# A hybrid decoder layer on one core: parked quarters of x in the idle k/q buffer, staggered block loads, and an in-place block inverse

## The chip, the core and the metric

The kernel runs on one core of a Trainium2 chip. The core has five engines with instruction streams of their own: TensorE (PE in the profile; its weight loads are PEld), VectorE (DVE), ScalarE (ACT), GpSimd (POOL) and SyncE (SP). Here SP and POOL mainly issue DMAs. The engines wait for one another through semaphores; within one engine the stream runs in order. The metric is device microseconds of one execution, lower is better.

## What is computed

One layer of a decoder trunk in float32, for a prompt of 1024 rows and 8 sample rows of 1024 channels. The reference, cut to its core:

```python
h = rmsnorm(x, norm_pre) * (1.0 + scale[:, None]) + shift[:, None]
proj = h @ w_in                                     # 1024 -> 10256 columns
hA, cA, bA, zA, qkv, zB, beta_raw, alpha_raw, gA, gB = jnp.split(proj, offs, axis=-1)
a_conv, new_buf_a = causal_dwconv(cA * hA, buf_a, conv_a_w)
yA = ((bA * a_conv) * jax.nn.silu(zA)) @ w_out_a
qkv_c, new_buf_b = causal_dwconv(qkv, buf_b, conv_b_w)
q, k, v = jnp.split(jax.nn.silu(qkv_c), [D_K, 2 * D_K], axis=-1)     # 8 heads of 128
...
a_mat = jnp.where(strict, jnp.einsum('bhncd,bhnsd->bhncs', kb, k) * decay, 0.0)
a_mat = a_mat + jnp.eye(C, dtype=jnp.float32)
sol = lax.linalg.triangular_solve(a_mat, rhs, left_side=True, lower=True, unit_diagonal=True)
...                                                 # a scan over the chunks of one head
o = rmsnorm(o, onorm_w) * jax.nn.silu(zB)
yB = o @ w_out_b
merged = jax.nn.sigmoid(gA) * yA + jax.nn.sigmoid(gB) * yB
y = x + gate[:, None] * rmsnorm(merged @ w_o, norm_post)
```

## The kernel before

**Stages.** (1) A startup computes the modulation and the normalised, transposed input x, kept in SBUF as a high and a low part, `xh` and `xl` (8 tiles of 128 channels by 1032 columns). Every product takes three matmuls (high by high, low by high, high by low). (2) Eight heads: for each head the jobs k, q, v, two gates and zB, each one 128-column slice of `w_in` against all of x, in three column groups. Beside them runs the delta rule of the head: `decay_gen`, `delta_gen`, and `sample_gen` for the sample rows. (3) Three groups of branch A, four jobs each. (4) `products()`: the five other groups of branch A as seven products each (P1, P2, P6, P7, P4, P5, P3) on quarters of x, a Strassen-like scheme. P1 and P2 read x as it stands; P6, P7 and P4 read the "parked" quarter combinations T2, T3 and T4 of x, and P5 reads T1, all of which `quarter_gen` computed and stored to the DRAM scratch `txs` during the heads. (5) The output products and the final norm.

**Order of the work.** The program text is written by a planner at build time. PE's jobs run in a fixed order; everything else is a "strand", a Python generator. After each matmul triple `slot()` (line 599) steps every strand whose model time lies behind PE's. `force(cond)` (line 612) steps strands with no matmul of the job between them until a condition holds. The tile framework then orders each engine's stream by readiness in a model of its own, with the place in the text as the priority, and sets the semaphores.

**Slots.** `T4` is a pool of `NT4 = 5` buffers of 128 by 1056 floats (class `Slots`, line 629), handed out first in, first out. During the heads these take slots: v of a head (`vT`), the split of k and q (`kqh`, `kql`, per half), the block inverse (`At`, `Tt`), the output `yb`, one gate row (`gate`, by `take`, which forces), the sample state (`S0`, `rB`), and `quarter_gen` (`qa`, `qb`, `qhi`, `qlo`). A strand that finds too few slots yields and asks again later.

**The block inverse.** `delta_gen` (line 864) stores the 32 by 32 diagonal blocks of a head to DRAM (`sA`) and reads all 32 of them back, one block a partition, into `At`. `Tt` is set to the identity by GpSimd, and 31 steps of two VectorE instructions each (`Ttmp` is the product) do a forward substitution. The result goes through DRAM (`sT`) into `Tn`, and matmuls then join the blocks into `U`. The chunk loop follows: eight chunks, each a chain between TensorE, ScalarE and VectorE, whose output gathers in `on`.

**Flags.** Head h's `delta_gen` begins once head h-2 is out ("out": its row of yB is stored), and its chunk loop once head h-1 is out. "done" is set earlier, when a head's chunk loop has ended. The buffer `kq` (k and q of a head) exists twice; k of head h waits for "done" of head h-2, and for heads 0 and 1 for nothing.

**Loads of the parked quarters.** `block_load` (line 1458) loads T2, T3 and T4, four DMAs each, from POOL into slots (`tx`) of the pool that takes over the heads' memory, and then T1 into the second half of `xh` and `xl`. The weights of the products come by DMAs from SP (`wr`).

In the profile nearly all instructions stand under one line, L122, the planner's wrapper; so instructions are told apart by the names of their tiles.

Of the kernel before, what the change touches and what calls it, by code (L numbers as in the profile page):

```python
# [8 lines left out]
F32 = mybir.dt.float32  # L9
# [3 lines left out]
ALU = mybir.AluOpType  # L13
# [3 lines left out]
P = 128  # L17
D = 1024
NK = 8
S = 1024  # L20
NB = 8
NT = S + NB
NH = 8
C = 128
NC = S // C
# [4 lines left out]
CY = S + 4 * NB  # L30
# [2 lines left out]
COL_H, COL_C, COL_B, COL_Z, COL_Q, COL_K, COL_V = 0, 1024, 2048, 3072, 4096, 5120, 6144  # L33
COL_ZB, COL_BA, COL_GA, COL_GB = 7168, 8192, 8208, 9232
BIG = 1.0e30
NT4 = 5
DYN = 2048
HT = NT // 2
PW = HT // 2
# [115 lines left out]
def hybrid_step(  # L155
# [23 lines left out]
    def tt(out, a, b, op):  # L179
        V.tensor_tensor(out=out, in0=a, in1=b, op=op)  # L180
# [7 lines left out]
    def stt(out, a, s, b, op0, op1):  # L188
        V.scalar_tensor_tensor(out=out, in0=a, scalar=s, in1=b, op0=op0, op1=op1)
# [64 lines left out]
    egc = cpool.tile([P, NC, NH], F32, name="egc")  # L254
# [14 lines left out]
    sA = dram.tile([NH, NC, 4, 32, 32], F32, name="sA")  # L269
# [334 lines left out]
    def start(gen):  # L604
        bg.append(Strand(gen, sched.cur.t if sched.cur else sched.clk["PE"]))
# [59 lines left out]
    def when(*conds):  # L665
        while not all(c() for c in conds):
            yield
# [124 lines left out]
    flags = {}  # L792
# [70 lines left out]

    def delta_gen(h, st):
        ch = lambda a: a[:, :, h:h + 1]
        while "DA" not in st or "v" not in st or (h > 1 and not flags.get(("out", h - 2))):
            yield
        kq, vT, gcB, DB, DA = st["kq"], st["v"], st["gcB"], st["DB"], st["DA"]
        V.tensor_copy(out=qs_s[:, h, :, 0], in_=smpl(kq[:, 0, :]))
# [7 lines left out]
        ssq = bp.tile([P, NC], F32, tag="ssq", name="ssq", bufs=2)  # L877
# [18 lines left out]
        rk = rsqrt(bp, ssk, P, NC, "rk")  # L896
        cB = bp.tile([P, NC], F32, tag="cB", name="cB", bufs=2)
        nx = bp.tile([P, NC], F32, tag="nx", name="nx", bufs=2)
        vs = bp.tile([P, NC], F32, tag="vs", name="vs", bufs=2)
        bh = beta[:, 0:NC, h]  # L900
        tt(vs, rk, bh, ALU.mult)
        tt(cB, vs, rk, ALU.mult)
        stt(nx, cB, -1.0, egc[:, :, h], ALU.mult, ALU.mult)
        yield

        for half in range(2):
# [25 lines left out]
        for b in range(4):  # L932
            sched.loose(b < 3)
            bs = slice(32 * b, 32 * b + 32)
            SY.dma_start(out=sA[h, :, b].rearrange("c r j -> r c j"), in_=DB[bs, :, bs])
        while not T4.ready(2):
            yield
        At_, Tt_ = T4.get("At", S), T4.get("Tt", S)
        At = At_[:32].rearrange("p (r j) -> p r j", j=32)
        Tf = Tt_[:32]  # L940
        Tt = Tf.rearrange("p (r j) -> p r j", j=32)
        tmp = bp.tile([32, 272], F32, tag="Ttmp", name="Ttmp")
        SY.dma_start(out=At, in_=sA[h].rearrange("c b r j -> (c b) r j"))
        sched.loose()
        GP.memset(Tf, 0.0)
        GP.memset(Tf[:, 0:1024:33], 1.0)
        sched.loose(False)
        t_at, sched.cur.t = sched.cur.t, t_kk
        vp = bp.tile([P, NC, C], F32, tag="vp", name="vp", bufs=2)
        for half in range(2):  # L950
# [14 lines left out]
        yield  # L965
        sched.cur.t = max(sched.cur.t, t_at)
        yield 0.0
        for j in range(31):
            n, w = 31 - j, j + 1
            tv = tmp[:, 0:n * w].rearrange("p (n w) -> p n w", w=w)  # L970
            tt(tv, At[:, j + 1:32, j:j + 1].to_broadcast([32, n, w]),
               Tt[:, j:j + 1, 0:w].to_broadcast([32, n, w]), ALU.mult)
            tt(Tt[:, j + 1:32, 0:w], Tt[:, j + 1:32, 0:w], tv, ALU.subtract)
            yield 0.0
        SY.dma_start(out=sT[h].rearrange("c b r j -> (c b) r j"), in_=Tt)
        T4.give(At_)
# [25 lines left out]
        for p in (0, 1):  # L1002
            b1 = slice(64 * p, 64 * p + 32)
            b2 = slice(64 * p + 32, 64 * p + 64)
            pt = ps_aux().rearrange("p (c j) -> p c j", j=64)
            for c in range(NC):
                PE.matmul(pt[b1, c, 0:32], lhsT=Tn[b1, c, :], rhs=Qs[b1, c, 0:32], start=True, stop=True)
            if p:
                A.mul(out=U[b1, :, b2], in_=pt[b1, :, 0:32], mul=-1.0)
# [6 lines left out]
            A.mul(out=U[b1, :, b2], in_=pt[b1, :, 0:32], mul=-1.0)  # L1016
            A.mul(out=T11[b2, :, 0:32], in_=pt2[b2, :, 0:32], mul=-1.0)
            yield 0.0
        pt = ps_aux().rearrange("p (c j) -> p c j", j=64)
        for c in range(NC):  # L1020
# [7 lines left out]
        A.mul(out=U[0:64, :, 64:128], in_=pt[0:64], mul=-1.0)  # L1028
# [48 lines left out]
        yield  # L1077
        tt(on, on, ro.unsqueeze(2).to_broadcast([P, NC, C]), ALU.mult)
        yield
        while "sz" not in st or not T4.ready():  # L1080
            yield
        sz = st["sz"]
        yb = T4.get("yb", S)
        for half in range(2):
            pt = ps_aux()
            for i in range(4):
# [4 lines left out]
            yield  # L1091
        sched.join("V")
        store(yBsc[h, :, 0:S], yb)
        T4.give(yb)
        flags[("out", h)] = True

    def head_jobs(h):
# [31 lines left out]
    L = []  # L1129
# [211 lines left out]
            yield  # L1341


    def quarter_gen():
        for k in range(4):
            yield from when(lambda: T4.ready(2))
            a, b = T4.get("qa", NT), T4.get("qb", NT)
            a1, a2, b1, b2 = a[:, 0:HT], a[:, HT:NT], b[:, 0:HT], b[:, HT:NT]
            tt(a, xh[:, k, :].bitcast(F32), xl[:, k, :].bitcast(F32), ALU.add)
            yield  # L1350
            tt(b, xh[:, 4 + k, :].bitcast(F32), xl[:, 4 + k, :].bitcast(F32), ALU.add)
            yield
            tt(a1, a2, a1, ALU.subtract)
            tt(a2, b2, a2, ALU.subtract)
            yield
            tt(b2, b2, a1, ALU.subtract)
            tt(b1, b1, b2, ALU.subtract)
            yield
            for r, v in enumerate((a, b)):
                yield from when(lambda: T4.ready(2))  # L1360
                hi, lo = T4.get("qhi", NT), T4.get("qlo", NT)
                A.copy(out=hi.bitcast(F32R), in_=v)
                yield
                tt(lo.bitcast(F32R), v, hi, ALU.subtract)
                T4.give(v)
                store(txs[r, 0, k].bitcast(F32), hi)
                store(txs[r, 1, k].bitcast(F32), lo)
                T4.give(hi)
                T4.give(lo)
                yield  # L1370
# [135 lines left out]
    def products():  # L1506
# [6 lines left out]
        for t in range(SG, NK):  # L1513
            tiles = [L[0].take("acc", NT) for _ in range(4)]
            for p in PROD:
# [284 lines left out]
```

## Time and profile before

| | us |
|---|---|
| median of 3 runs (lowest, highest) | 1494.98 (1494.11, 1499.9) |
| the profiled execution, whole | 1496.61 |
| its span, first to last instruction | 1494.6 |
| TensorE busy in the span | 1423.4 (95%) |
| VectorE busy | 947.8 (63%) |
| ScalarE busy | 645.1 (43%) |
| GpSimd busy | 42.0 (3%) |

The views used below: the page's 40 slices give the busy share in tenths; the table of stages gives, for each stretch, its length, then busy us (and instructions) of PE, PEld, DVE, ACT and POOL, then the granted TensorE clock, the DMA share and GB/s; the timeline gives start, length, engine, line, operation, written and read tiles, sizes, and in brackets the idle time before the instruction and what ended it; the view of a tile gives shortest, median and longest instruction in ns and the first and last start in us.

### The profile page before, as it was taken

What the parts mean: (1) busy time and instruction counts of PE and PEld (TensorE: products, weight loads), DVE (VectorE), ACT (ScalarE), POOL (GpSimd) and SP (SyncE); (2) the same over time, 40 slices, a digit from 0 to 9 for tenths busy, and PEclk for the clock granted to TensorE, in tenths of its full rate; (3) what the DMA queues carried; (4) which work ended last, traced back from release to release, by engine and by line L of the source; (5) the groups of instructions that cost most, each with busy time, mean ns of one, the idle gap of its engine ahead of it and who ended that gap; (6) DMA issues with size and microseconds to landing.
All of it is one profiled execution on the core that took longest, in us unless ns stands there. A gap on an engine that the chain in (4) does not pass through costs nothing.

```text
span 1494.6 us, 25637 instructions
## 1 busy us (share of the span) xinstructions
PE 1423.4 (95%) x10050; PEld 1362.3 (91%) x10050; DVE 947.8 (63%) x2391; ACT 645.1 (43%) x1512; POOL 42.0 (3%) x73
## 2 busy tenths in 40 slices
PE   6999959989999999999999999959999999999997
PEld 4899959979999999999999999959999989999786
DVE  6865868849559578595776824227767773444553
ACT  6765634645547438465383332112323462332221
POOL 0000000000000001000000000020000000000000
PEclk9999979989999999999999999979999999999999
DMA  9624222214332322223222312094121474451221
GB/s 321 165 60 145 89 79 80 79 54 159 92 84 77 96 75 80 79 80 100 65 80 66 89 52 73 15 308 112 48 71 58 139 257 138 155 166 42 89 85 57
DMA packets 182542, 155.42 MB, mean 104 GB/s; under 512 B 25405, under 2 KB 161063, under 8 KB 182414
## 3 DMA queue, kind: packets, MB, share of 16 engines
q1 hardware_dynamic: 177900, 145.26, 32.5%
q0 software_dynamic: 4320, 8.46, 1.8%
q8 instruction: 79, 1.29, 0.3%
q14 instruction: 41, 0.34, 0.1%
q10 hardware_dynamic: 202, 0.08, 0.0%
HBM read 117.08 MB, written 36.91 MB: 103 GB/s over the span
## 4 chain that ended last, share of the span: by engine, by line
PE 75%; DVE 10%; DMA 7%; ACT 4%; SPq 2%; issue 2%; DVEq 0%; ACTq 0%
PE pm_t L122 57%; PE pa_t L122 16%; SPq L122 2%; DVE kq L122 2%; DMA gcB<-gsc 2%; PE pb L122 2%; DVE Tt L122 2%; DVE Ttmp L122 2%; DVE wlo L122 1%; DMA xs<-in_x_prompt_dram 1%; ACT junk L122 1%; DMA aw<-in_ada_w_dram 1%; ACT L122 1%; DMA txs<-qlo 1%; DVE vT L122 1%
## 5 line engine op out<-in xcount | busy, mean ns | idle before, releaser
L122 PE MATMUL pm_t<-xh,whi 128*128 128x344 f32 (+1 forms) x1576 | 520.6, 330 | 18.8 <-ACT gate L122 17.1
L122 PE MATMUL pm_t<-xh,wlo 128*128 128x344 f32 (+1 forms) x1576 | 500.7, 318 | 0.6 <-DVE wlo L122 0.6
L122 PE MATMUL pm_t<-xl,whi 128*128 128x344 f32 (+1 forms) x1576 | 499.8, 317 | 0.0
L122 PEld LDWEIGHTS pm_t<-xh,whi 128*128 128x128 f32 x1576 | 298.8, 190 | 21.7 <-ACT gate L122 17.7
L122 PEld LDWEIGHTS pm_t<-xh,wlo 128*128 128x128 f32 x1576 | 297.9, 189 | 1.1 <-DVE wlo L122 0.9
L122 PEld LDWEIGHTS pm_t<-xl,whi 128*128 128x128 f32 x1576 | 298.5, 189 | 0.1
L122 DVE TENSOR_TENSOR wlo<-wraw,whi 128x512 fp32r<-128x512 f32 x152 | 102.1, 683 | 61.5 <-ACT whi L122 61.2
L122 ACT CAST whi<-wraw 128x512 fp32r<-128x512 f32 x152 | 91.5, 622 | 105.2 <-PE pm_t L122 104.9
L122 PE MATMUL pm_t<-ylo,whi 128*128 128x344 f32 x384 | 123.4, 321 | 1.8 <-DVE ylo L122 1.8
L122 PE MATMUL pm_t<-yhi,whi 128*128 128x344 f32 x384 | 123.2, 322 | 0.6 <-DVE acc L122 0.6
L122 PE MATMUL pm_t<-yhi,wlo 128*128 128x344 f32 x384 | 123.6, 322 | 0.0
L122 DVE TENSOR_TENSOR Ttmp<-At,Tt 32x31 f32<-32x31 f32 (+15 forms) x248 | 81.4, 328 | 7.0 <-DMA At<-sA 2.2
L122 DVE TENSOR_TENSOR Tt<-Tt,Ttmp 32x31 f32<-32x31 f32 (+15 forms) x248 | 81.7, 329 | 5.1
L122 PEld LDWEIGHTS pm_t<-ylo,whi 128*128 128x128 f32 x384 | 72.6, 189 | 2.2 <-DVE ylo L122 2.1
L122 PEld LDWEIGHTS pm_t<-yhi,whi 128*128 128x128 f32 x384 | 72.7, 190 | 1.2 <-issue 0.8
L122 PEld LDWEIGHTS pm_t<-yhi,wlo 128*128 128x128 f32 x384 | 72.6, 189 | 0.0
L122 DVE SCALAR_TENSOR_TENSOR kq<-raw,vecs,kq 128x528 f32<-128x528 f32 x96 | 69.6, 757 | 1.3 <-ACT kq L122 1.1
L122 PE MATMUL pm_t<-tx,whi 128*128 128x258 f32 x256 | 48.3, 291 | 18.0 <-ACT whi L122 18.0
L122 ACT CAST whi<-wr 128x1024 fp32r<-128x1024 f32 x26 | 27.3, 1049 | 79.9 <-PE pm_t L122 37.3
L122 PEld LDWEIGHTS pm_t<-tx,whi 128*128 128x128 f32 x256 | 41.1, 197 | 18.2 <-issue 18.2
L122 ACT ACTIVATE junk<-pa_t 128x128 f32<-128x128 f32 x192 | 53.9, 281 | 8.5 <-PE pa_t L122 5.6
L122 ACT COPY vn<-pa_t 128x128 f32<-128x128 f32 x64 | 17.1, 267 | 84.3 <-PE pa_t L122 83.9
(367 smaller groups left out, 2575.7 us busy)
## 6 DMA issues: line engine op xcount, KB each, us to landing
wraw<-in_w_in_dram SPq DMA_DIRECT2D x60, 512.0 KB
wr<-in_w_in_dram SPq DMA_DIRECT2D x36, 256.0 KB
aw<-in_ada_w_dram SPq DMA_DIRECT2D x16, 512.0 KB
tx<-txs POOLq DMA_DIRECT2D x12, 516.0 KB, 12.4
txs<-qhi SPq DMA_DIRECT2D x8, 516.0 KB
txs<-qlo SPq DMA_DIRECT2D x8, 516.0 KB
gBsc<-gate SPq DMA_DIRECT2D x8, 516.0 KB
gAsc<-gate SPq DMA_DIRECT2D x8, 516.0 KB
```

Source lines behind the costliest of these rows:

```text
L122: r = f(*args, **kw)
```

## The change

- `NT4` goes from 5 to 6. The output `on` of the chunk loop is no buffer of its own any more; it takes a slot, and `yb` is written into the same slot, which goes back when the row is stored.
- `quarter_gen` no longer takes slots for its two combinations: it is given one of the two `kq` buffers (the one that head 1 takes later), is started before the job that follows the startup instead of after the beta/alpha product, and takes slots for `qhi` and `qlo` only.
- The block inverse works in place: the sign moves into `cB`, the blocks are loaded straight into `Tt`, there are 30 steps, each one column narrower, and VectorE sets the diagonal in the middle. `At` and the two GpSimd memsets are gone, and three `A.mul` by -1 become copies.
- `delta_gen` of head h begins on "done" of head h-2, and its chunk loop on "out" of head h-2 and a free slot. `ssq` has three buffers.
- `block_load` asks for T2, T3, T4 and T1 not before units 0, 1, 2 and 3 of the products (`unit[0]` counts products).
- The load of yB rows for the output product starts one product earlier (at P6 of the last group, not P7).

```diff
-NT4 = 5
+NT4 = 6
...
-        while "DA" not in st or "v" not in st or (h > 1 and not flags.get(("out", h - 2))):
+        while "DA" not in st or "v" not in st or (h > 1 and not flags.get(("done", h - 2))):
...
-        tt(cB, vs, rk, ALU.mult)
-        stt(nx, cB, -1.0, egc[:, :, h], ALU.mult, ALU.mult)
+        stt(cB, vs, -1.0, rk, ALU.mult, ALU.mult)
+        tt(nx, cB, egc[:, :, h], ALU.mult)
...
-        while not T4.ready(2):
+        while not T4.ready():
             yield
-        At_, Tt_ = T4.get("At", S), T4.get("Tt", S)
-        At = At_[:32].rearrange("p (r j) -> p r j", j=32)
+        Tt_ = T4.get("Tt", S)
...
-        SY.dma_start(out=At, in_=sA[h].rearrange("c b r j -> (c b) r j"))
-        sched.loose()
-        GP.memset(Tf, 0.0)
-        GP.memset(Tf[:, 0:1024:33], 1.0)
-        sched.loose(False)
+        SY.dma_start(out=Tt, in_=sA[h].rearrange("c b r j -> (c b) r j"))
...
-        for j in range(31):
-            n, w = 31 - j, j + 1
-            tv = tmp[:, 0:n * w].rearrange("p (n w) -> p n w", w=w)
-            tt(tv, At[:, j + 1:32, j:j + 1].to_broadcast([32, n, w]),
-               Tt[:, j:j + 1, 0:w].to_broadcast([32, n, w]), ALU.mult)
-            tt(Tt[:, j + 1:32, 0:w], Tt[:, j + 1:32, 0:w], tv, ALU.subtract)
+        for j in range(1, 31):
+            n = 31 - j
+            tv = tmp[:, 0:n * j].rearrange("p (n w) -> p n w", w=j)
+            tt(tv, Tt[:, j + 1:32, j:j + 1].to_broadcast([32, n, j]),
+               Tt[:, j:j + 1, 0:j].to_broadcast([32, n, j]), ALU.mult)
+            tt(Tt[:, j + 1:32, 0:j], Tt[:, j + 1:32, 0:j], tv, ALU.add)
+            if j == 15:
+                sched.loose()
+                V.memset(Tf[:, 0:1024:33], 1.0)
+                sched.loose(False)
             yield 0.0
...
-        while h and not flags.get(("out", h - 1)):
-            yield
-        on = bp.tile([P, NC, C], F32, tag="on", name="on")
+        while (h > 1 and not flags.get(("out", h - 2))) or not T4.ready():
+            yield
+        on_ = T4.get("on", S)
+        on = on_.rearrange("p (c d) -> p c d", d=C)
...
-        yb = T4.get("yb", S)
+        yb = on_
...
-    def quarter_gen():
+    def quarter_gen(q_):
         for k in range(4):
-            yield from when(lambda: T4.ready(2))
-            a, b = T4.get("qa", NT), T4.get("qb", NT)
+            a, b = q_[:, 0, 0:NT], q_[:, 1, 0:NT]
...
-        for b, r, cs in (("T2", 1, slice(HT, NT)), ("T3", 0, slice(HT, NT)), ("T4", 1, slice(0, HT))):
-            yield from when(lambda: L, lambda: L[0].ready(4))
+        for i, (b, r, cs) in enumerate((("T2", 1, slice(HT, NT)), ("T3", 0, slice(HT, NT)), ("T4", 1, slice(0, HT)))):
+            yield from when(lambda: L, lambda: L[0].ready(4), lambda: unit[0] >= i)
...
+        yield from when(lambda: unit[0] >= 3)
         for part, x_ in enumerate((xh, xl)):
...
-                    if p == "P7":
+                    if p == "P6":
                         start(load_rows("yb", yBsc))
...
+    start(quarter_gen(bp.tile([P, 2, CY], F32, tag="kq", name="kqq", bufs=2)))
     jobs[0][6]()
...
-    start(quarter_gen())
```

More of the change, by code (lines that the diff above doesn't have):

```diff
@@ L876, in delta_gen @@
         ssk = bp.tile([P, NC], F32, tag="ssk", name="ssk", bufs=2)
-        ssq = bp.tile([P, NC], F32, tag="ssq", name="ssq", bufs=2)
+        ssq = bp.tile([P, NC], F32, tag="ssq", name="ssq", bufs=3)
         for src, sq in ((0, ssk), (1, ssq)):
@@ L935, in delta_gen @@
             SY.dma_start(out=sA[h, :, b].rearrange("c r j -> r c j"), in_=DB[bs, :, bs])
-        while not T4.ready(2):
+        while not T4.ready():
             yield
-        At_, Tt_ = T4.get("At", S), T4.get("Tt", S)
-        At = At_[:32].rearrange("p (r j) -> p r j", j=32)
+        Tt_ = T4.get("Tt", S)
         Tf = Tt_[:32]
         Tt = Tf.rearrange("p (r j) -> p r j", j=32)
-        tmp = bp.tile([32, 272], F32, tag="Ttmp", name="Ttmp")
-        SY.dma_start(out=At, in_=sA[h].rearrange("c b r j -> (c b) r j"))
-        sched.loose()
-        GP.memset(Tf, 0.0)
-        GP.memset(Tf[:, 0:1024:33], 1.0)
-        sched.loose(False)
+        tmp = bp.tile([32, 256], F32, tag="Ttmp", name="Ttmp")
+        SY.dma_start(out=Tt, in_=sA[h].rearrange("c b r j -> (c b) r j"))
         t_at, sched.cur.t = sched.cur.t, t_kk
@@ L967, in delta_gen @@
         yield 0.0
-        for j in range(31):
-            n, w = 31 - j, j + 1
-            tv = tmp[:, 0:n * w].rearrange("p (n w) -> p n w", w=w)
-            tt(tv, At[:, j + 1:32, j:j + 1].to_broadcast([32, n, w]),
-               Tt[:, j:j + 1, 0:w].to_broadcast([32, n, w]), ALU.mult)
-            tt(Tt[:, j + 1:32, 0:w], Tt[:, j + 1:32, 0:w], tv, ALU.subtract)
+        for j in range(1, 31):
[8 more added lines that the diff above has]
+                sched.loose(False)
             yield 0.0
         SY.dma_start(out=sT[h].rearrange("c b r j -> (c b) r j"), in_=Tt)
-        T4.give(At_)
         T4.give(Tt_)
@@ L1008, in delta_gen @@
             if p:
-                A.mul(out=U[b1, :, b2], in_=pt[b1, :, 0:32], mul=-1.0)
+                A.copy(out=U[b1, :, b2], in_=pt[b1, :, 0:32])
                 yield
@@ L1015, in delta_gen @@
             sched.loose()
-            A.mul(out=U[b1, :, b2], in_=pt[b1, :, 0:32], mul=-1.0)
-            A.mul(out=T11[b2, :, 0:32], in_=pt2[b2, :, 0:32], mul=-1.0)
+            A.copy(out=U[b1, :, b2], in_=pt[b1, :, 0:32])
+            A.copy(out=T11[b2, :, 0:32], in_=pt2[b2, :, 0:32])
             yield 0.0
@@ L1027, in delta_gen @@
             PE.matmul(pt[0:64, c, :], lhsT=T11[:, c, :], rhs=Qs[0:64, c, :], start=True, stop=True)
-        A.mul(out=U[0:64, :, 64:128], in_=pt[0:64], mul=-1.0)
+        A.copy(out=U[0:64, :, 64:128], in_=pt[0:64])
         yield
-        while h and not flags.get(("out", h - 1)):
+        while (h > 1 and not flags.get(("out", h - 2))) or not T4.ready():
             yield
-        on = bp.tile([P, NC, C], F32, tag="on", name="on")
+        on_ = T4.get("on", S)
+        on = on_.rearrange("p (c d) -> p c d", d=C)
         so = bp.tile([P, NC], F32, tag="so", name="so", bufs=2)
@@ L1079, in delta_gen @@
         yield
-        while "sz" not in st or not T4.ready():
+        while "sz" not in st:
             yield
         sz = st["sz"]
-        yb = T4.get("yb", S)
+        yb = on_
         for half in range(2):
@@ L1093, in delta_gen @@
         store(yBsc[h, :, 0:S], yb)
-        T4.give(yb)
+        T4.give(on_)
         flags[("out", h)] = True
@@ L1364, in quarter_gen @@
                 tt(lo.bitcast(F32R), v, hi, ALU.subtract)
-                T4.give(v)
                 store(txs[r, 0, k].bitcast(F32), hi)
```

## The prediction

> **What bounds the kernel now.** I read the page's 40 slices first, then the table of stages, then the list of TensorE's waits, then the timelines around the two longest.
>
> ```profile
> span 1494.6 us, 25637 instructions
> PE   6999959989999999999999999959999999999997
> PEclk9999979989999999999999999979999999999999
> ...
> 175.00:225.00 50.00, 32.90 (x279) 31.35 (x278) 35.77 (x105) 20.28 (x60) 0.21 (x1) 0.80 0.23 71
> 300.00:350.00 50.00, 44.19 (x278) 39.49 (x278) 28.73 (x84) 26.45 (x68) 1.09 (x2) 0.90 0.33 106
> 350.00:975.00 625.00, 623.04 (x4635) 607.94 (x4635) 403.75 (x1192) 290.80 (x811) 21.02 (x25) 1.00 0.27 77
> 975.00:1025.00 50.00, 30.77 (x237) 30.24 (x236) 19.46 (x27) 7.46 (x13) 8.46 (x12) 0.80 0.95 273
> ...
> PE pm_t L122 <- ACT whi L122: 18.0, 1, 18.0
> PE pm_t L122 <- ACT gate L122: 17.1, 1, 17.1
> ```
>
> The kernel is bound by TensorE: from 350 to 975 us it is idle for 2 us of 625, with six heads passing. Shortening VectorE or ScalarE work there is worth nothing. What can be won is in three places: 17.1 us of idle in 175 to 225, 5.8 in 300 to 350 and 19.2 in 975 to 1025, each with a clock below 1. Two single waits make most of it: one on a gate row (ScalarE), one on `whi`, the split weights of a product. So the question for each edit is whether it ends one of these.
>
> **The gate wait** (TensorE, ScalarE, VectorE; head 0's inverse):
>
> ```profile
> 188.62 0.32 PE L122 MATMUL pm_t<-xl,whi 128*128 128x344 f32 x1
> 188.78 0.32 PE L122 MATMUL pm_t<-xh,wlo 128*128 128x344 f32 x1
> 206.21 0.65 PE L122 MATMUL pm_t<-xh,whi 128*128 128x344 f32 x1 [17.10 <-ACT gate L122]
> ...
> 211.24 0.49 PE L122 MATMUL pm_t<-xh,wlo 128*128 128x344 f32 x1
> ...
> 205.71 1.14 ACT L122 COPY gate<-pm_t 128x344 f32<-128x344 f32 x3 [19.36 <-DVE Ttmp L122]
> ...
> 174.02 0.19 DVE L122 TENSOR_TENSOR Ttmp<-At,Tt 32x31 f32<-32x31 f32 x1
> ...
> 205.49 0.18 DVE L122 TENSOR_TENSOR Ttmp<-At,Tt 32x31 f32<-32x31 f32 x1
> ...
> 137.59 1.82 SPq L122 DMA_DIRECT2D sA<-DB  x4
> 163.38 0.44 SPq L122 DMA_DIRECT2D At<-sA  x1
> 167.52 1.15 POOL L122 MEMSET Tt<- 32x1024 f32 x2 [10.05 <-DVE qlo L122]
> ```
>
> The gate copy has its PSUM long ready; it waits until the last `Ttmp` has read `At`, because its slot is the one that `At` gives up. Four PSUM buffers fill, and TensorE stops. The inverse itself is late for the same reason: the blocks were stored by 139 us, but the load into `At` went out at 163.4, and the memset of `Tt` at 167.5, behind a `qlo` in whose slot it lies. Slots are short because of the quarters:
>
> ```profile
> L122 DVE TENSOR_TENSOR qa<-xh,xl x4: 1169/1228/1234, 58.7 to 239.8; 128x1032 f32<-128x1032 f32 x4
> L122 DVE TENSOR_TENSOR qlo<-qb,qhi x4: 1214/1222/1232, 72.9 to 356.7; 128x1032 fp32r<-128x1032 f32 x4
> ...
> 74.17 1.23 DVE L122 TENSOR_TENSOR qa<-xh,xl 128x1032 f32<-128x1032 f32 x1
> ...
> 62.00:152.00 90.00, 87.96 (x575) 84.96 (x576) 56.25 (x138) 57.46 (x123) 0.96 (x3) 1.00 0.37 112
> 152.63 4.17 DVE L122 SCALAR_TENSOR_TENSOR kq<-raw,vecs,kq 128x528 f32<-128x528 f32 x6 [0.19 <-ACT kq L122]
> ```
>
> The first quarter took from 58.7 to 74.2 us, the last ended at 358. In between `qa` and `qb` hold two of the five slots; with `At`, `Tt` and head 1's v that is all five at 186 us.
>
> **Term A, the gate wait.** The change takes out `qa`, `qb` and `At` and adds a slot. At 186 us there would be `Tt` and v of head 1, perhaps `kqh`, `kql` and `on`: at most five of six, so the gate finds one. Gain 17.1 us, and the slow stretch behind it: 17 intervals from 206.21 to 211.24 at 0.296 us against 0.16 (188.62 to 188.78) are 2.3 us. Together 19.4. The Trainium skill, page "TensorE: Matmul & The Clock Gate", section "What's actually happening", says that an idle window of about 3.4 us halves the clock and about 3.4 us of work restores it; by that figure the loss would be half of 3.4, an estimate of 1.7 us, and A 18.8. The trace shows half speed for 5.0 us, so the row decides. What is late next? VectorE, which also carries weight splits; while TensorE stood still it ran the inverse. Head 0's inverse can now begin soon after its blocks are stored, some 25 us earlier, so less of it meets head 1's convolutions. If nothing of that cover came, A would lose at most what the old stall gave VectorE, so A lies between 0 and 19.4; I take 19.4, since the releaser is named in the row.
>
> **Term B, 300 to 350 us.**
>
> ```profile
> 300.00:305.00 5.00, 5.00 (x30) 4.42 (x29) 0.87 (x6) 0.58 (x1) 0.00 (x0) 0.54 0.00 0
> 305.00:310.00 5.00, 5.00 (x29) 4.60 (x28) 0.97 (x2) 1.99 (x4) 0.00 (x0) 0.50 0.00 1
> ...
> 315.00:320.00 5.00, 4.35 (x28) 3.45 (x27) 3.33 (x13) 3.86 (x16) 0.00 (x0) 1.00 0.00 0
> 320.00:325.00 5.00, 3.34 (x20) 2.50 (x20) 2.27 (x5) 2.00 (x6) 0.00 (x0) 1.00 0.35 105
> 325.00:330.00 5.00, 3.42 (x27) 3.03 (x26) 4.53 (x11) 1.77 (x5) 0.00 (x0) 1.00 0.01 3
> ...
> 330.53 0.80 ACT L122 COPY gate<-pm_t 128x344 f32<-128x344 f32 x2 [0.45 <-PE pa_t L122]
> ```
>
> From 315 to 330 head 1's chunk loop runs with almost no job matmuls between its links, and then a gate row is copied: this is what `force` for a slot looks like when the planner itself runs out. The fourth quarter still holds slots there. Idle 0.65 + 1.66 + 1.58 = 3.9 us, which I count as won (bounds 0 and the stage's 5.8). The ten microseconds at about half clock cost (1 - 0.52) x 10 = 4.8 us; they follow a crowd of small matmuls that every head has, and six later heads pass at clock 1.00. Either end is possible (0 to 4.8); I take half, 2.4.
>
> **Term C, the parked loads.** Code order does not hold a DMA back here:
>
> ```profile
> 971.04 0.87 POOL L122 DMA_DIRECT2D xl<-txs  x1 [175.10 <-PE pm_t L122]
> ...
> 981.84 4.93 POOL L122 DMA_DIRECT2D tx<-txs  x7 [9.18 <-DMA yAsc<-hA]
> ...
> 995.56 0.72 POOL L122 DMA_DIRECT2D tx<-txs  x1 [1.21 <-issue]
> ...
> 997.13 1.23 DVE L122 TENSOR_TENSOR wsum<-wr 128x1024 f32<-128x1024 f32 x1 [13.78 <-DMA wr<-in_w_in_dram]
> ...
> 1002.26 1.42 PE L122 MATMUL pm_t<-tx,whi 128*128 128x258 f32 x5 [18.02 <-ACT whi L122]
> ...
> L122 SPq DMA_DIRECT2D yraw<-yBsc x8: 319/330/383, 1124.6 to 1203.3; - x8
> ```
>
> The text puts T1 (`xl`) last, after T4, yet POOL issued it first, at 971, when its target came free; and the first yB row was fetched at 1124.6, some 40 us before the product that starts it (P6 and P7 of the last group lie around 1167 and 1173, seven products of 5.8 us back from 1196). POOL's stream has nothing else to do, so a load that stands later in the text is issued as soon as its slot is free. All twelve `tx` go out between 981.8 and 996, and nothing in the new conditions is a wait on the chip. The 18.0 us wait for `whi`, whose inputs (`wr`) share the DMA engines with them, stays: 0. Bounds: -8 to +2. If only T2 (2.1 MB) and the two weight tiles that P6 needs (1.0 MB) moved first, at the stage's 273 GB/s they would take 11.5 us from 981.8, landing at 993.3 instead of 997.1, 3.8 us sooner; with T1's 2 MB out of the way of the row store `yAsc<-hA`, which frees POOL at 981.8, some 2 to 4 us more. The Trainium skill, "DMA: Bandwidth & Descriptors", section "Issuing engines are not separate DMA queues", says that DMAs of all issuers share 16 engines and interleave; by it a stagger that took effect would pay, and by these rows it does not take effect.
>
> **Term D, yB rows one product earlier.** Bounds 0 and 1.8 us (the wait below), for the load is fetched early already. I take 0.
>
> ```profile
> 1203.76 0.42 PE L122 MATMUL pm_t<-ylo,whi 128*128 128x344 f32 x1 [1.83 <-DVE ylo L122]
> ...
> L122 DVE TENSOR_TENSOR Ttmp<-At,Tt 32x31 f32<-32x31 f32 (+15 forms) x248 | 81.4, 328 | 7.0 <-DMA At<-sA 2.2
> L122 ACT COPY on<-pa_t x64: 244/266/291, 225.3 to 908.3; 128x128 f32<-128x128 f32 x64
> L122 SPq DMA_DIRECT2D yBsc<-yb x8: 319/326/339, 267.4 to 918.9; - x8
> ```
>
> **Term E, the inverse.** 62 instructions a head become 60, over 2 x 496 fewer elements. From 31 elements at 0.19 us and the mean of 328 ns at 176 elements, an element costs about 0.95 ns and an instruction 0.16 us apart from them: 0.94 + 0.32 = 1.3 us a head, 10 us of VectorE in all. TensorE has other work in six of eight heads (350 to 975), and in the first two the slots were the limit: 0. Without TensorE's cover it would be the whole 10. The diagonal is one small memset moved to VectorE; POOL loses two per head, and nobody waited for those but the inverse. The copies in place of `A.mul` are the same ScalarE instructions in number and size, and the flags of head h-2 only loosen the order: 0.
>
> **Term F, what is added.** Three quarters' work moves ahead of 152 us. A quarter is four full VectorE instructions at 1.23 and four halves, about 7.6 us; nearly two of the four were done by then, so about 16 us are moved into a stretch where VectorE is idle for 33.8 of 90. The `txs` stores that come with them (516 KB each) meet a DMA share of 0.37. So 0, with up to 3 us if weight splits are late. `on` now holds a slot from a head's first chunk to its stored row, 225.3 to 267.4 in head 0: 42 us against the At it replaces, about as long (163.4 to 205.7), so the load on slots is no higher, and there is one slot more.
>
> **Sum.** 19.4 + 3.9 + 2.4 = 25.7 us off the profiled execution, 1496.6 (span 1494.6 and 2.0 around it): 1470.9. The median of the runs is 1.6 below the profiled one, so 1469.3.
>
> **Rivals.** *The stagger works as well*: C is worth 8, 1461. For it: DMA share 0.95 in that stage. Against: the order of the rows above. *Half is given back*: VectorE or a new short force takes part of A and B; 13 us remain, about 1482. For it: VectorE was 36 of 50 us busy in 175 to 225, and those 50 become some 31. *Slower: the quarter ends late*. Head 1's k is written at 151 to 153 us into the buffer that `quarter_gen` uses, and nothing in the text makes it wait for that; the tile order does. Behind that first write on ScalarE stand all PSUM copies, so every microsecond beyond TensorE's four PSUM buffers (three column groups of 24 x 0.157, about 11 us) stops it. At 15.5 us a quarter, four take from 59 to 121, so there are 30 us to spare. It decides if a quarter takes over 26 us: at the old pace (four by 358) the stall would be 358 - 152 - 11 = 195 us; slower than before begins at 11 + 26 = 37 us late; an end at 200 would be 48 late, stall 37 and give 1506. *The change does not do what it says for slots*: 1495.
>
> **Chances.** Forecast 0.56 (its own range 1460 to 1480), stagger 0.12, half given back 0.20 (of which 0.08 within the bound), slower 0.08, nothing 0.04. A measurement of this kernel tells about 0.5% from no change: faster is below 1487.5. Faster 0.56 + 0.12 + 0.12 = 0.80, same 0.12, slower 0.08. The range leaves out the slower case, nothing, and the ends of the others: 1457 to 1488.
>
> **What would show it.** Right: no TensorE wait above 3 us between 120 and 350; head 0's inverse starts near 145; the last `qlo` ends before 150; no gate copy behind `Ttmp`. C right: POOL still issues all twelve `tx` within about 15 us, and TensorE waits some 18 us for `whi` near 958. Wrong: a wait of that size for `whi` gone (stagger), a ScalarE `kq` write held behind `qlo` near 152 (slower), or gate copies released by `on` or `yb`.

## The result, and the profile after

| | before | after |
|---|---|---|
| median of 4 runs each (lowest, highest) | 1495.95 (1494.11, 1499.9) | 1475.03 (1472.51, 1479.06) |
| ratio, 95% interval | | 0.9859, 0.9827 to 0.9892 |
| the profiled execution, whole (span) | 1496.61 (1494.6) | 1472.51 (1470.4) |

The change takes 1.4% off. The span fell by 24.2 us, where the sum of the prediction said 25.7. But the profiled execution is the fastest of the four: the median fell by 20.9, to 1475.0 where the forecast was 1469.3. The four lie at 1472.5, 1473.3, 1476.8 and 1479.1 us, with a mean granted clock of 0.991, 0.991, 0.986 and 0.984, so the kernel's own spread of 6.6 us goes with the clock.

The same views as before, of the changed kernel: the span and two rows of the page's 40 slices, the table of stages (length, busy us and instructions of PE, PEld, DVE, ACT, POOL, clock, DMA share, GB/s), and TensorE's waits (total, times, longest).

```profile
span 1470.4 us, 25580 instructions
PE   6999899999999999999999999959999999999997
...
PEclk9999999999999999999999999979999999999999
```

```profile
175.00:225.00 50.00, 47.46 (x304) 47.39 (x305) 40.01 (x120) 26.19 (x69) 5.52 (x3) 0.97 0.36 101
300.00:350.00 50.00, 50.00 (x341) 46.70 (x339) 34.77 (x118) 28.13 (x91) 0.00 (x0) 1.00 0.34 80
350.00:955.00 605.00, 597.68 (x4472) 584.57 (x4472) 383.32 (x1147) 279.20 (x792) 16.23 (x15) 1.00 0.28 76
955.00:1005.00 50.00, 30.27 (x235) 29.73 (x234) 19.69 (x28) 7.47 (x13) 8.46 (x12) 0.83 0.94 270
```

```profile
PE pm_t L122 <- ACT whi L122: 18.3, 1, 18.3
PE pm_t L122 <- ACT gate L122: 7.1, 3, 4.7
...
PE pa_t L122 <- DVE X L122: 4.2, 2, 2.1
PE pa_t L122 <- DVE sm_r L122: 3.2, 1, 3.2
```

The gate wait of 17.1 is gone, and 300 to 350 is full at clock 1.00. The start of the products is as it was, 18.3 us of waiting for `whi`. New are small waits: a gate wait of 4.7 at 177, 3.2 us at 278 and 283 (another gate wait and one for `raw`), and 7.3 us of idle between 350 and 955 where there were 2.0 (3.2 for `sm_r` at 353, the rest for X).

**The gate wait of 4.7** is head 1's k held behind the last quarter. Timelines of VectorE, ScalarE and TensorE:

```profile
68.30 2.37 DVE L122 TENSOR_TENSOR qlo<-kqq,qhi 128x1032 fp32r<-128x1032 f32 x2
79.36 1.24 DVE L122 TENSOR_TENSOR qlo<-kqq,qhi 128x1032 fp32r<-128x1032 f32 x1
113.82 1.23 DVE L122 TENSOR_TENSOR qlo<-kqq,qhi 128x1032 fp32r<-128x1032 f32 x1
148.25 1.23 DVE L122 TENSOR_TENSOR qlo<-kqq,qhi 128x1032 fp32r<-128x1032 f32 x1
...
173.61 1.22 DVE L122 TENSOR_TENSOR qlo<-kqq,qhi 128x1032 fp32r<-128x1032 f32 x1
```

```profile
174.92 2.24 ACT L122 ACTIVATE kq<-raw,vecs 128x1056 f32<-128x1056 f32 x2 [2.73 <-DVE qlo L122]
177.07 0.42 ACT L122 COPY gate<-pm_t 128x344 f32<-128x344 f32 x1
```

```profile
177.54 0.66 PE L122 MATMUL pm_t<-xh,whi 128*128 128x344 f32 x1 [4.75 <-ACT gate L122]
```

Each quarter has two `qlo` (the low parts of its two halves). The first quarter was through at 70.7, but the second's two came at 79.4 and 113.8, the third's first at 148.3, and the last of all ended at 174.8, not at 121. The buffer they use is head 1's `kq`, so its first write waits on ScalarE, and the gate copy that TensorE needs is next in ScalarE's stream.

**The waits for X** (at 513.5 and 698.1, alike; here the first):

```profile
512.55 0.19 DVE L122 TENSOR_TENSOR Ttmp<-Tt 32x30 f32<-32x30 f32 x1 [3.26 <-DMA Tt<-sA]
...
513.15 0.33 DVE L122 SCALAR_TENSOR_TENSOR X<-pa_t,nx,vp 128x128 f32<-128x128 f32 x1
```

```profile
513.53 0.49 PE L122 MATMUL pa_t<-X,U 128*128 128x128 f32 x2 [2.08 <-DVE X L122]
```

VectorE stands 3.3 us before the first step of the next head's inverse, whose blocks are still in flight, and the X of the running chunk loop is queued behind it.

### The profile page after: what moved, and what is told of

Read it like the earlier page. It is cut to its first block, busy times and chain, and to the rows that moved or that the text cites. A ratio compares the mean times of both kernels' runs of the same rounds, so it can differ in the third digit from the quotient of the medians.

```text
span 1470.4 us, 25580 instructions
## 1 busy us (share of the span) xinstructions
PE 1414.5 (96%) x10050; PEld 1356.0 (92%) x10050; DVE 936.9 (64%) x2383; ACT 643.2 (44%) x1512; POOL 44.4 (3%) x57
## 5 line engine op out<-in xcount | busy, mean ns | idle before, releaser
L122 DVE TENSOR_TENSOR Ttmp<-Tt 32x30 f32<-32x30 f32 (+14 forms) x240 | 76.0, 317 | 14.9 <-DMA Tt<-sA 10.7
L122 DVE TENSOR_TENSOR Tt<-Tt,Ttmp 32x30 f32<-32x30 f32 (+14 forms) x240 | 76.1, 317 | 4.2
L122 PE MATMUL pm_t<-tx,whi 128*128 128x258 f32 x256 | 48.0, 290 | 18.3 <-ACT whi L122 18.3
## 6 DMA issues: line engine op xcount, KB each, us to landing
tx<-txs POOLq DMA_DIRECT2D x12, 516.0 KB, 12.6
txs<-qhi SPq DMA_DIRECT2D x8, 516.0 KB
txs<-qlo SPq DMA_DIRECT2D x8, 516.0 KB
gBsc<-gate SPq DMA_DIRECT2D x8, 516.0 KB
gAsc<-gate SPq DMA_DIRECT2D x8, 516.0 KB
```

Of the source, the lines that this page charges most:

```text
L122: r = f(*args, **kw)
```

## The experiments

Each kernel was timed beside the kernel before on the same chip, but not all on one chip, so kernels are best compared by the ratio. To read them, one sum per profiled execution was made from the table of stages in stretches of 5 us, from 62 us to the start of the last `szA` copy (`szA` belongs to branch A's three groups, ahead of the products): idle is the sum of length less TensorE's busy time; clock loss is the sum of busy time by (1 - clock). The stretch less both is 869 to 875 us in all fourteen kernels, so the two columns hold most of what differs ahead of the products. One execution stands for each kernel here, so a few us of clock loss can be chance.

| kernel | median us | ratio (95%) | last `szA` | idle | clock loss |
|---|---|---|---|---|---|
| before | 1495.95 | 1 | 973.6 | 28.9 | 8.1 |
| changed | 1475.03 | 0.9859 (0.9827 to 0.9892) | 953.2 | 15.5 | 2.9 |
| e1, rows late | 1480.20 | 0.9897 (0.9877 to 0.9917) | 959.6 | 15.9 | 9.3 |
| e2, five slots | 1468.02 | 0.9823 (0.9802 to 0.9845) | 951.0 | 11.9 | 4.9 |
| e3, quarters in slots | 1467.20 | 0.9815 (0.9795 to 0.9835) | 948.4 | 11.6 | 4.5 |
| e4, gated loads | 1475.46 | 0.9876 (0.9851 to 0.9900) | 955.2 | 14.8 | 5.8 |
| e5, before + inverse | 1463.09 | 0.9792 (0.9775 to 0.9809) | 942.3 | 7.4 | 2.9 |
| e6, old inverse | 1462.40 | 0.9789 (0.9772 to 0.9806) | 943.1 | 6.6 | 1.7 |
| e7, e2 and e3 | 1472.25 | 0.9850 (0.9835 to 0.9865) | 954.7 | 15.2 | 4.8 |
| e8, lo in place | 1477.35 | 0.9883 (0.9869 to 0.9898) | 960.0 | 15.8 | 6.9 |
| e9, inverse behind X | 1476.39 | 0.9869 (0.9837 to 0.9900) | 956.6 | 13.7 | 8.0 |
| e10, k after quarters | 1459.83 | 0.9765 (0.9747 to 0.9783) | 940.9 | 8.1 | 1.7 |
| e11, e5 + rows + gates | 1462.05 | 0.9780 (0.9760 to 0.9800) | 942.1 | 7.9 | 2.7 |
| e12, e6 and e10 | 1469.34 | 0.9829 (0.9812 to 0.9845) | 950.0 | 10.0 | 9.2 |

### The parts of the change, undone one by one

**e1, the load of yB rows.**

```diff
-                    if p == "P6":
+                    if p == "P7":
                         start(load_rows("yb", yBsc))
```

> The changed kernel with the load of the yB rows put back to P7 of the last group, one product later. The prediction (step D: rows are fetched early anyway) expects no difference, 1475 within 2 us. The rival, read from the trace after the change (the span gained 24.2 us but the products start only 20.1 us earlier, so 4 us were won behind them), expects 3 to 4 us more, 1478 to 1479, with a TensorE wait on ylo near 1184 and a half-clock stretch behind it.

Measured: 1480.2, 5 us more by the medians (the intervals overlap), near what the rival said; yet not for its reason. The first and last start of the `szA` copies, changed kernel and e1:

```profile
L122 ACT ACTIVATE szA<-pm_t x9: 450/457/459, 837.8 to 953.2; 128x344 f32<-128x344 f32 x9
```

```profile
L122 ACT ACTIVATE szA<-pm_t x9: 451/457/458, 844.2 to 959.6; 128x344 f32<-128x344 f32 x9
```

e1 is 6.4 us late already at 953, some 200 us ahead of the edit, and TensorE's instructions come in the same order in both up to there. The clock makes the 6.4 (9.3 against 2.9). Stages of TensorE alone (length, busy, clock, DMA share, GB/s), changed kernel and e1:

```profile
245.00:250.00 5.00, 5.00 (x85) 1.00 0.53 136
250.00:255.00 5.00, 5.00 (x40) 1.00 0.01 3
255.00:260.00 5.00, 5.00 (x37) 1.00 0.00 0
```

```profile
245.00:250.00 5.00, 5.00 (x93) 0.81 0.78 212
250.00:255.00 5.00, 5.00 (x32) 0.50 0.00 1
255.00:260.00 5.00, 5.00 (x27) 0.66 0.01 3
```

From the last `szA` to the end the changed kernel takes 1470.4 - 953.2 = 517.2 and e1 1478.2 - 959.6 = 518.6, 1.4 us more, with the 1.8 us wait for `ylo` back in e1's list of waits. The wait is the edit's: before, e1 and e5, the three kernels that load the rows late, have it (1.8, 1.8 and 1.4), and no other kernel has. The 1.4 us as a time is not clear of chance, for the same stretch takes 516.0 to 519.4 in the kernels that load the rows early.

**e2, e3, e7, slots and quarters.** The edits are `NT4 = 5`, and the old `quarter_gen` (two slots `qa` and `qb`, started after the beta/alpha product); e7 has both.

> The changed kernel with five slots instead of six; all else as changed. The prediction (step A: qa, qb, At out and one slot more, at most five of six taken at the gate) expects that five would do or nearly: at 186 us Tt, v of head 1 and at most kqh, kql and on; so 1475 to 1480 and no gate wait over 6 us before 350. The rival, that the sixth slot carries the gain, expects most of the 20 us back: 1488 to 1495, with a gate copy behind on, Tt or qlo.

> The changed kernel with quarter_gen back in two slots of its own and started after the beta/alpha product, as before; six slots, in-place inverse. If the quarters' two slots were what starved the gate (prediction, steps A and B), the idle time of 175 to 225 and of 300 to 350 comes back in part: 1482 to 1492. If the sixth slot and the missing At were enough, 1470 to 1476, and the 4.75 us gate wait at 177 (head 1's k behind the last quarter) is gone.

> The changed kernel with both others undone: five slots, and quarter_gen in two slots of its own, started late as before; in-place inverse and on in a slot as changed. Theory that At carries the gain: 1466 to 1474, like each undone alone (1468, 1467). Rival, that either one of the two is needed to replace the slot that on now takes: the gate wait returns, 1480 or more.

Measured: 1468.0, 1467.2 and 1472.3; e2 and e3 lie below every range that was expected. No gate wait above 3.4 us came back in any of them. The sixth slot is not needed, nor is the quarters' move: without the move the kernel is 8 us faster by the medians (the intervals overlap by a little). In e7 a wait of 8.5 us for `raw` stands at 283. That e2 is faster than the changed kernel is not shown: the intervals overlap, and the profiled spans are both 1470.4.

**e5, e6, the inverse.** e5 is the kernel before with the hunks of the inverse alone; e6 is the changed kernel with these hunks taken back. The core, as e5 has it:

```diff
-        while not T4.ready(2):
+        while not T4.ready():
             yield
-        At_, Tt_ = T4.get("At", S), T4.get("Tt", S)
...
+        Tt_ = T4.get("Tt", S)
```

> The kernel before with the in-place block inverse alone: At gone, Tt loaded straight, one slot a head instead of two; five slots, quarter_gen in slots, on in a buffer of its own, old flags, old loads. Theory after the first four runs (the slot At is what the gate row waited for; the quarters' move and the sixth slot are not needed): the 17.1 us gate wait goes or falls below 5, 1468 to 1476. Rival (the prediction's step A, where qa, qb, At and one slot more act together): five slots with qa and qb held still starve the gate, 1485 to 1495.

> The changed kernel with the old block inverse back (At and Tt, two slots, GpSimd memsets, 31 steps); six slots, quarters in the k/q buffer and all the rest as changed. Theory that the in-place inverse carries the gain: a gate or another wait of 10 us or more between 150 and 350 comes back, 1485 to 1495. Rival (enough slots by any of the three edits): within 3 of the changed kernel, 1472 to 1478; step E alone, 11 us less of VectorE work, is covered by TensorE.

Measured: 1463.1 and 1462.4. This is the main result. The inverse alone takes 32 us off the kernel before (1495.3 beside it), more than the whole change; and the change without the inverse does the same. Both expectations of e6 fell, on the good side. In the lists of TensorE's waits, e5 and e6, the 17.1 us are gone from both:

```profile
PE pm_t L122 <- ACT gate L122: 1.3, 1, 1.3
```

```profile
PE pm_t L122 <- ACT gate L122: 3.9, 4, 1.3
```

So either way of freeing slots ends the 17.1 us wait. Together they win nothing more: the changed kernel is 10 to 13 us slower than either (spans 1470.4 against 1460.0 and 1459.5), and 8 to 9 of that is idle time ahead of the products (15.5 against 7.4 and 6.6).

**The conditions of `block_load`** need no run: the program built without them has the same instructions in the same order in every engine's stream.

### The load at the start of the products

**e4, a real wait.** GpSimd copies a column of the split weight source into each target of T3 and T4 ahead of its DMA, so that the DMA waits for it, and a column of T4 ahead of T1.

```diff
+                    if i:
+                        yield from when(lambda: "w" in gate_src)
+                        GP.tensor_copy(out=v[:, 0:1].bitcast(F32R), in_=gate_src["w"][:, 0:1])
                     GP.dma_start(out=v.rearrange("p (k n) -> p k n", k=2).bitcast(F32R),
...
+            GP.tensor_copy(out=x_[:, 0, HT:HT + 1], in_=blocks["T4"][part][:, 0:1])
             GP.dma_start(out=x_[:, 0:4, HT:NT], in_=txs[0, part, :, :, 0:HT].rearrange("k p n -> p k n"))
```

> The changed kernel with a real wait on the chip for the parked loads: before each DMA of T3 and T4 GpSimd copies one column of the first group's split weight source into the target, and before T1 one column of T4, so that T2 and the weights have the DMA engines first. Prediction, bounds of step C: the 18.3 us wait for whi shrinks by 4 to 8 us, 1467 to 1471. Rival: the wait is set by the store that frees the memory and not by the sharing, 1475, wait still 17 to 18; a wait for T3 or T4 may take its place.

Measured: 1475.5, no difference. The wait did shrink, and another came. Timelines of TensorE and GpSimd, and stages of TensorE:

```profile
977.45 1.41 PE L122 MATMUL pm_t<-tx,whi 128*128 128x258 f32 x5 [11.54 <-ACT whi L122]
```

```profile
976.34 4.10 POOL L122 CAST tx<-wq 128x1 fp32r<-128x1 f32 x8 [12.04 <-DVE wq L122]
980.38 5.05 POOL L122 DMA_DIRECT2D tx<-txs  x7
```

```profile
985.00:990.00 5.00, 1.07 (x6) 0.82 1.31 393
990.00:995.00 5.00, 5.00 (x25) 0.50 1.24 361
```

The wait for `whi` is 6.7 us shorter, but T3, asked for only at 980, is late for P7 at 985: 3.9 us of idle and a second stretch at half clock. So the loads that share the DMA engines do lengthen the wait for `whi`, and what is held back is late itself; the DMA share is above 1 in both rows.

**e11, an earlier gate**, on e5 with the rows early: T3 waits only for the last weights to land, T4 for the split source.

> The kernel before with the in-place inverse (1463 alone), the yB rows one product earlier, and parked loads held on the chip: T3 until the last weights of the first group have landed, T4 until the split source is made, T1 behind T4. Sum of the single results: 1463, less 2 to 5 for the rows, less 3 to 6 for the loads if T3 no longer comes late as it did with the later gate (then the wait for whi shrank from 18.3 to 11.5 but 3.9 on tx came back with a second half-clock stretch): 1453 to 1460. If the DMA engines are simply full, T3 is late again and the loads give nothing: 1459 to 1463.

Measured: 1462.05 against e5's 1463.09, intervals overlapping. The wait for `whi` is 12.2 instead of 17.3 and T3 is in time, but 2.6 us of waiting for `wlo` follow at 982, and the span is only 1.8 us shorter in all, with the end of the wait for `ylo` (1.4 in e5) in it. The higher hope, 1453 to 1460, fell.

### The new waits

**e8, the quarters shortened.** The low part is written over the quarter and stored from there, so one slot does.

```diff
-                yield from when(lambda: T4.ready(2))
-                hi, lo = T4.get("qhi", NT), T4.get("qlo", NT)
+                yield from when(T4.ready)
+                hi = T4.get("qhi", NT)
...
-                tt(lo.bitcast(F32R), v, hi, ALU.subtract)
+                tt(v.bitcast(F32R), v, hi, ALU.subtract)
```

> The changed kernel with the low part of each quarter written over the quarter itself in the k/q buffer and stored from there, so that quarter_gen takes one slot at a time and not two. If the 4.7 us gate wait at 177 us comes from quarters that end late for want of slots (the second waited from 114 to 148), the last quarter ends before 160 and the wait goes: 1468 to 1471. Rival: VectorE's stream or the stores hold the quarters, the wait stays, 1474 to 1477.

Measured: 1477.35. The last quarter ends at 166, 9 us sooner but not before 160, and the gate wait is down to 0.5. But TensorE stands at the same place, now for `raw`, and only 0.8 us less. ScalarE and TensorE of e8:

```profile
172.15 2.24 ACT L122 ACTIVATE kq<-raw,vecs 128x1056 f32<-128x1056 f32 x2 [5.80 <-DVE Tt L122]
```

```profile
177.43 0.65 PE L122 MATMUL pm_t<-xh,whi 128*128 128x344 f32 x1 [3.91 <-ACT raw L122]
```

k's write comes 2.8 us sooner, not 9: the last low part now leaves from the lent buffer itself, by a store that goes out at 165.9. Whether the write waits for that store or, as the row has it, for VectorE is not settled. Later come 2.1 us more for `raw`, 2.4 for `whi` and 2.4 for `ro_a`, and the clock loss is 6.9. So slots were a part of the quarters' delay: the second quarter's two `qlo` are 7 us apart here and not 34. The third still starts its high part at 136.1, against 135.4 in the changed kernel.

**e10, the text told of the buffer's owner.** Head 1's k is written, in the text too, only when the quarters have ended.

```diff
-                lambda: h < 2 or flags.get(("done", h - 2)), kdst,
+                lambda: flags.get("quarters") if h == 1 else h < 2 or flags.get(("done", h - 2)), kdst,
```

> The changed kernel, but head 1's k waits in the text too until quarter_gen has ended, so that the order is made with the end of the quarters known. If the 4.75 us gate wait at 177 is head 1's k write standing on ScalarE behind the last qlo with the gate copy behind it, the wait falls below 2 and the time by 3 to 6 (half clock with it), 1469 to 1472. Rival: k simply comes later and the raw buffers run out instead, a wait of 4 or more on raw, 1475 or above.

Measured: 1459.8, by the median the fastest kernel of the study (its interval overlaps with those of e5, e6 and e11), 15 us below the changed one and 2.35% below before (0.9765, 0.9747 to 0.9783). The last `qlo` of both, changed and e10, and e10's ScalarE:

```profile
L122 DVE TENSOR_TENSOR qlo<-kqq,qhi x8: 1211/1228/1235, 68.3 to 173.6; 128x1032 fp32r<-128x1032 f32 x8
```

```profile
L122 DVE TENSOR_TENSOR qlo<-kqq,qhi x8: 1212/1224/1233, 68.9 to 167.3; 128x1032 fp32r<-128x1032 f32 x8
```

```profile
168.64 2.25 ACT L122 ACTIVATE kq<-raw,vecs 128x1056 f32<-128x1056 f32 x2 [3.65 <-DVE qlo L122]
...
173.36 0.45 ACT L122 COPY gate<-pm_t 128x344 f32<-128x344 f32 x1 [1.45 <-PE pm_t L122]
```

k is written 6.3 us sooner, and the gate copy is ready before TensorE asks (`1.45 <-PE`). In e10's list of TensorE's waits:

```profile
PE pa_t L122 <- DVE X L122: 6.4, 3, 3.1
...
PE pm_t L122 <- ACT gate L122: 0.5, 1, 0.5
```

Of the 12.4 us of span, gate waits are 6.6 (7.1 to 0.5) and `sm_r` 3.2 (it isn't in the list any more), less 2.2 that X takes back (4.2 to 6.4); the clock gives 1.2, and 3.6 are left over, in TensorE's busy time. So the wait that the edit was made for is 4.2 of it (4.7 to 0.5); that the rest also hangs on k's write is not shown.

**e9, X ahead of the inverse.** In heads 4 and 6 the inverse starts 4 us later in the text, and two one-column copies hold it behind X.

```diff
-        sched.cur.t = max(sched.cur.t, t_at)
+        sched.cur.t = max(sched.cur.t, t_at + (4000.0 if h in (4, 6) else 0.0))
         yield 0.0
+        if h in (4, 6):
+            V.tensor_copy(out=tmp[:, 0:1], in_=flags["X"][:32, 0:1])
+            V.tensor_copy(out=Tf[:, 0:1], in_=flags["X"][:32, 0:1])
```

> The changed kernel, but in heads 4 and 6 the first step of the inverse is started 4 us later in the text and held behind the X of the running chunk loop by two one-column copies of X (into Ttmp and into a diagonal element that is overwritten later). In the changed kernel VectorE waits 3.3 us at 512.6 and again at 697.1 for the DMA Tt<-sA with X queued behind it, and TensorE waits 2.1 us for X each time. If that is the price of the early inverse, both waits on X go and the time falls by about 4, to 1470 to 1472. Rival: the chunk loop has no cover there and the wait only moves to the next link, 1474 to 1477.

Measured: 1476.4, no difference from the changed kernel. The waits on X are gone, and waits on S, the next link, of 3.2 us are there: the rival holds. TensorE's stream has two matmul triples of a job between one link and the next there, and they end before S comes; moving the stop along the chain takes 1 us off the waits (4.2 to 3.2).

**e12, both cures.** e6 and the line of e10.

> The changed kernel with head 1's k waiting in the text for the quarters (1460 alone) and the old block inverse in two slots (1462 alone). If the 6.4 us of waits on X that are left with the first edit belong to the in-place inverse (its first step stands at the head of VectorE's stream for the DMA Tt<-sA, with X behind), they go, and the time is 1453 to 1457. If both edits cure the same thing, head 1's k with the gate copy behind it, the gains don't add: 1458 to 1463.

Measured: 1469.3, worse than either, which neither theory said. A new wait of 6.1 us for `Un` at 218 (the inverse on its way back from DRAM) is followed by 20 us at or near half clock. One X wait of 2.4 is left, so the X waits are not the in-place inverse's alone; e5 and e7 have that inverse too, and wait 0.7 or less for X.

## Why the prediction came out, step by step

Of the four signs that the prediction named for being right, one came: no gate copy stands behind `Ttmp` any more. The others failed: a TensorE wait of 4.75 us at 177, head 0's inverse at 162.3 and not near 145, the last `qlo` ending at 174.8 and not before 150. One of its signs of being wrong, a `kq` write held behind `qlo`, is there. Both signs for term C came. The forecast holds as a sum, and in part by luck.

**A, the gate wait: right.** 17.1 us and the half clock behind it went; the 4.75 that came instead belong to F, and so does about 1 us of clock from 175 to 185. But the reason was counted too wide: `qa` and `qb`, `At` and the sixth slot are not needed together. The inverse alone does it (e5), and so do slot and quarters without it (e6).

**B: right for the loop, the clock under-sized by half.** 300 to 350 is full at clock 1.00, but it is not the same work: head 1's chunk loop now runs from about 250 to 273, with job matmuls between its links, and its idle time is gone. Just behind it TensorE now waits 2.2 us for a gate copy and 1.1 for `raw`:

```profile
278.07 0.42 PE L122 MATMUL pm_t<-xh,whi 128*128 128x344 f32 x1 [2.17 <-ACT gate L122]
```

The whole 4.8 of clock came, not 2.4. It isn't the change's to keep: e1 and e9 run the same instructions up to there and lose some 5 us of clock at 245 to 260.

**C: right.** POOL's order is the same, T1 first, and the wait for `whi` is 18.3:

```profile
950.65 0.87 POOL L122 DMA_DIRECT2D xl<-txs  x1 [224.79 <-PE pm_t L122]
...
961.32 4.93 POOL L122 DMA_DIRECT2D tx<-txs  x7 [9.05 <-DMA yAsc<-hA]
```

The price set for a real stagger (up to 8) did not come as a gain: in e4 the wait for `whi` fell by 6.7 and the time was given back to T3, in e11 it fell by 5.1 and 2.6 came back at `wlo`.

**D: inside its bounds** (0 to 1.8), but not 0: the wait for `ylo` hangs on the edit (e1), though its 1.4 us are within the spread of that stretch.

**E: right in size, wrong on the start.** VectorE has 11 us less, against 10:

```profile
L122 DVE TENSOR_TENSOR Ttmp<-Tt 32x30 f32<-32x30 f32 (+14 forms) x240 | 76.0, 317 | 14.9 <-DMA Tt<-sA 10.7
```

```profile
162.28 0.19 DVE L122 TENSOR_TENSOR Ttmp<-Tt 32x30 f32<-32x30 f32 x1
```

```profile
150.00:200.00 50.00, 45.95 (x101) 0.97 0.47 152
```

76.0 for `Ttmp` where 81.4 stood, and as much less for `Tt`. But head 0's inverse started at 162.3 and not near 145, and the waits of all heads for their blocks rose from 2.2 to 10.7 us. The blocks themselves left late: on SyncE's queue the last of them had gone out at 153.3, and at 139.4 in the kernel before.

```profile
152.95 0.31 SPq L122 DMA_DIRECT2D sA<-DB  x1
...
155.75 0.66 SPq L122 DMA_DIRECT2D Tt<-sA  x1
```

The move of the quarters does much of it. In the four kernels that leave them in slots and have the new inverse (e3, e5, e7, e11) head 0's inverse starts at 150.5 to 154.0, in the nine with moved quarters at 159.3 to 166.2. VectorE, which writes `DB` and is 46 of 50 us busy between 150 and 200 (the row of stages above, VectorE alone), is the "next late" that term A named and took at nothing.

**F: the step that failed.** "At 15.5 us a quarter, four take from 59 to 121, so there are 30 us to spare" (from the rival of the late quarter, on which term F rests): the pace was read off the first quarter, which found its slots free. The second quarter's two low parts lie 34 us apart, the third's first comes 34 us behind them, the last ended at 174.8, and the rival's mechanism (head 1's k held on ScalarE) set in. By the rival's own sum an end at 174.8 gives 174.8 - 152 - 11 = 11.8 us of stall; it was 4.75, where term F was 0, with 3 at most.

And the late end does not make the wait by itself. In e6 the last `qlo` starts at 174.7 and in e2 at 177.8, both later than here, and k is written behind it; yet TensorE waits 0.9 us or less for a gate copy there, for one stands ahead of k in ScalarE's stream. ScalarE of e6:

```profile
173.19 0.44 ACT L122 COPY gate<-pm_t 128x344 f32<-128x344 f32 x1
176.00 2.25 ACT L122 ACTIVATE kq<-raw,vecs 128x1056 f32<-128x1056 f32 x2 [2.37 <-DVE qlo L122]
178.15 0.42 ACT L122 COPY gate<-pm_t 128x344 f32<-128x344 f32 x1
```

So it is the late quarter together with the order of k's write and the gate copy that stops TensorE. e10, in which the quarters end and k is written 6.3 us sooner, is 12 to 15 us faster in all, but only the 4.2 of this wait are traced to it.

**The sum** came out because errors met, which is luck. Ahead of the products 21.0 us of idle were to go and 13.4 went (28.9 to 15.5); of clock 4.7 were to go and 5.2 went. What lacked in idle was made up by 3.8 behind the last `szA` (521.0 to 517.2; the wait for `ylo` is 1.8 of it, the rest not assigned) and 2.0 in TensorE's busy time. And this is the fastest execution of four: by the medians 20.9 us came where 25.7 were to come.

**What stays open**: which order of a chunk loop and the next inverse leaves which wait. Nine kernels have no gate wait above 3.4 us and lie between 1460 and 1477, and single cures don't add (e12); the experiments show where each one stands, not a rule for it.

## What to carry to other kernels

If several edits free the same resource, time each alone: here either one paid in full, and both together were 10 to 13 us slower than one. When a buffer is lent to another strand, let the order of the text know the real end of the loan, or the wait can appear at the head of an engine's queue with unrelated work behind it. And before a difference is put down to an edit, see whether it is there ahead of the edit, in idle time or in the clock.

## What the hardware showed unexpectedly

The clock falls to half with TensorE counted as busy. In e1 a crowd of 32 by 32 matmuls precedes it:

```profile
244.67 1.09 PE L122 MATMUL pa_t<-Un,DB 32*32 32x32 f32 x32
```

The changed kernel runs the same instructions at 1.00. In e1 the three stretches from 245 to 260 run at 0.81, 0.50 and 0.66, in e9 at 0.75, 0.50 and 0.72, with TensorE busy 5.00 us of 5.00 in each. So the same stream costs 5 us more in one execution than in another, a third of a per cent. The Trainium skill, "TensorE: Matmul & The Clock Gate", section "What's actually happening", describes an activity window that runs freely against the kernel; that it hits in some executions only agrees with these rows, while an idle engine, which the page names as the cause, is not what they show: what counts as idle in a crowd of small matmuls stays open.

GpSimd's issue of DMAs can be held back: in the changed kernel seven `tx` go out in 4.93 us from 961.3, and the other five, one each 1.9 us, take until 976. Busy DMA engines alone don't explain it: in e11, at a DMA share of 1.09 to 1.24, four go out in 2.89 us from 961.4 and four more in 2.88 us from 967.4. How many are under way may decide; no run here varies that alone.
